# An encoder kernel's opening on a transposed input, weight differences one block earlier, and a last quarter in two column halves

## The chip, the cores and the metric

One core of one Trainium2 chip. The metric is device time in microseconds of one execution: every input is in the chip's DRAM at the start, and the output must be there at the end.

## The reference

Two layers on 256 tokens of width 1024, all in float32. Each layer is a half-step feed-forward network (FFN), a mixing part with two attentions, and a second half-step FFN. The diff touches the FFNs, the opening ahead of the first and the end of the last; the mixing part is left as it was.

```python
D_MODEL, SEQ, DEPTH, D_FF = 1024, 256, 2, 2816

def rms_norm(x, g):
    return x * lax.rsqrt(jnp.mean(x * x, axis=-1, keepdims=True) + EPS) * g

def swiglu(x, w_gate, w_up, w_down):
    return (jax.nn.silu(x @ w_gate) * (x @ w_up)) @ w_down

for l in range(DEPTH):
    x = x + 0.5 * swiglu(rms_norm(x, ffn1_norm[l]), ffn1_w_gate[l], ffn1_w_up[l], ffn1_w_down[l])
    z = rms_norm(x, mix_norm[l]) @ w_in[l]
    ...
    x = x + merged @ w_out[l]
    x = x + 0.5 * swiglu(rms_norm(x, ffn2_norm[l]), ffn2_w_gate[l], ffn2_w_up[l], ffn2_w_down[l])
```

## The kernel before, in words

**Precision.** Every matrix is cut in a high part (rounded to the matmul's type) and a low part (the rest), and every product takes three matmuls: high by high, high by low, low by high (`three`, L193 to L196). ACT makes the high part by a copy, DVE the low part by a subtraction (`start_split`, L208 and L209). For weights these are `wh` and `wl`, made from a `raw` tile that a DMA brought; for activations `xh0`, `xl0` (tokens 0 to 127, "t0") and `xh1`, `xl1` (tokens 128 to 255, "t1").

**Norm.** The gain is multiplied into the transposed activations (`norm_steps`: four transposes on TensorE, a multiplication, a split). The scale of each token, 1/sqrt(mean square), is applied after the projection, when gate and up are combined: ACT computes the squares' sums (`square`), DVE two small steps on `ms`, POOL the power (`rs_y`, L200).

**An FFN** runs over 11 blocks of 512 columns (256 of gate, 256 of up). A block has 1024 rows of weights, in four pieces of two 128-row chunks each; TensorE takes 24 matmuls of 512 columns for each half of the tokens. `glu` (L480, L481) then computes the gating: ACT takes silu of the gate half, DVE multiplies by the up half, into `hh`. `send` turns `hh` over by a transposing DMA, `arrive` takes it back, adds and subtracts its quarters (tile `a`), and splits the result.

**Down projection.** Blocks are paired with their rows of the down matrix in a scheme with seven products of half the size instead of eight: names "1" to "7". Its weight side takes differences of the down matrix's rows (`sums`, tile `uv`, three instructions on DVE) and a split corner (`keep_corner`). The products of one pair, except "1", run among the matmuls of the block that follows (`quad`). The last blocks' rows are multiplied plainly at the end (`down_end`), a quarter of the output at a time: names "2", "3", "4" and "8".

**The first block of pairs** is block 3 of an FFN that opens a layer's first half (`first_quad`), and block 2 in the second FFN of a layer. The block ahead of it, c == first_quad - 1, fetches the first rows (`fetch_rows(0)`) and begins three pieces of the next block.

**The opening.** The first FFN of layer 0 has no earlier work to hide its loads. `opening` fetches x in four quarters, the gains of all norms in front of the first (HEAD columns), and block 0's four pieces. TensorE runs matmuls on a blank tile (`warmup`) between the first transposes.

**Order.** TensorE's order is the program's. The other engines' order comes from a scheduler that works with estimated times, except where `linked` ties an instruction behind the last one of the same engine in `chain`; between `chain[...] = ...` and `chain.clear()` a stretch of ACT's or DVE's work stands in the order in which it is written. `defer` holds a piece of work back until TensorE has done so many more units. SP issues the loads of weights and x in order, POOL the loads of small constants (`constants`, L105 to L107), behind the second norm's power. `behind` only sets an order between two loads.

**Buffers.** `raw` has 4, `wh` and `wl` 6 each, `rows` 2. The projection's PSUM tiles `g` have 2 banks.

Of the kernel before, what the change touches and what calls it, by code (L numbers as in the profile page):

```python
# [23 lines left out]
P = 128  # L24
# [27 lines left out]
IN_W = 4352  # L52
HEAD = 128
HELD = 3
# [5 lines left out]
@with_exitstack  # L60
def hybrid_encoder(ctx, tc, x, w_gu1, w_d1, w_in, b_gate, qk_gain, rpb, sink, t5,
                   w_bna, w_bsw, w_out, w_gu2, w_d2, c_mask, c_band, out):
# [17 lines left out]

    def fetch(t, h):
        if (t, h) == (0, 0):
            nc.sync.dma_start(wide[:, :HEAD + 512], x[:P, :HEAD + 512])
        else:
            nc.sync.dma_start(xs[t][:, h * 512:(h + 1) * 512],
                              x[t * P:(t + 1) * P, HEAD + h * 512:HEAD + (h + 1) * 512])

    fetch(0, 0)

# [44 lines left out]

    last_load, last_hi = [None], [None]

# [70 lines left out]
    def start_split(hi, lo, src):  # L207
        last_hi[0] = linked("act", lambda: nc.scalar.activation(hi, src, AF.Copy))  # L208
        return lambda: linked("dve", lambda: nc.vector.tensor_tensor(lo, src, hi.bitcast(F32), ALU.subtract))  # L209

    def split_to(hi, lo, src):
        start_split(hi, lo, src)()
# [6 lines left out]

    def norm_steps(t, n, half, apart=False):  # L220
        if half == 0:
            xT[t] = [act.tile([P, KD, P], F32R, name=f"x{p}{t}", tag=f"x{p}{t}") for p in "hl"]
            ssq[t] = small.tile([P, 2], F32, name="ssq", tag="ssq")
# [6 lines left out]
        if apart and half == 1:  # L230
            for i in range(4):
                linked("act", lambda: nc.scalar.activation(xg[:, i, :], tp[:, i, :], AF.Copy,
                                                           scale=gain[:, n, 4 + i:5 + i]))
        else:
            linked("dve", lambda: nc.vector.tensor_tensor(
                xg, tp, gain[:, n, ks].unsqueeze(2).to_broadcast([P, 4, P]), ALU.mult))
        yield
        split_to(*(x[:, ks, :] for x in xT[t]), xg)
        yield
        if not apart:  # L240
            square(t, half)

    def norm(t, n, half, apart=False):
        for _ in norm_steps(t, n, half, apart):
            pass
# [11 lines left out]

    def opening(w, l, early):
        ps = [ps_g.tile([P, 512], F32, name="g", tag="g") for _ in range(T)]

        def steps(t, i):
            wh, wl = pieces[i]
            xh, xl = xT[t]
            for a, b in ((xh, wh), (xl, wh), (xh, wl)):
                for k in (2 * i, 2 * i + 1):
                    nc.tensor.matmul(ps[t], a[:, k, :], b[:, k % 2, :], start=a is xh and b is wh and k == 0,  # L266
                                     stop=b is wl and k == KD - 1)
            tick(2)

        pieces = []  # L270
        chain["act"] = warmed
        warmup(5)
        norm(0, 0, 0, True)
        pieces.append(piece(w, l, 0, 0, 512))
        warmup(5)
        fetch(1, 0)
        norm(1, 0, 0, True)
        pieces.append(piece(w, l, 1, 0, 512))
        fetch(0, 1)
        fetch(1, 1)  # L280
        warmup(3)
        steps(0, 0)
        norm(0, 0, 1, True)
        steps(1, 0)
        pieces.append(piece(w, l, 2, 0, 512))
        norm(1, 0, 1, True)
        pieces.append(piece(w, l, 3, 0, 512))
        square(0, 0, idle)
        square(0, 1, idle)
        for i in (1, 2, 3):  # L290
            for t in range(T):
                steps(t, i)
        second = [piece(w, l, 0, 512, 512)]
        square(1, 0, idle)
        early(ps[0])
        second.append(piece(w, l, 1, 512, 512))
        square(1, 1, idle)
        second += [piece(w, l, i, 512, 512) for i in range(2, KD // 2)]
        chain.clear()
        defer(24, "constants", constants)  # L300
        defer(70, "scaled", scaled)
        return ps, second

# [52 lines left out]
    def ffn(l, n, w_gu, w_d, after, early, begun):  # L356
        first_quad = 2 if n else 3
        QUADS = NFC - first_quad
        with tc.tile_pool(name="ffn", bufs=1) as fp:
            on_way, rows_of, corner, hs, one = [], {}, {}, {}, {}  # L360

            def send(c, hh):
                z = fp.tile([P, 8 * P], U16, name="z", tag="z")
# [69 lines left out]
            def down_end(rest, start):  # L433
# [70 lines left out]
            for c in range(NFC):  # L504
                first = n == 0 and c == 0
                pair = [None]
                if first:
                    both, second = opening(w_gu, l, lambda ps: glu(0, ps, pair))
                    glu(1, both[1], pair)
                    send(c, pair[0])  # L510
                    continue
                if c < first_quad:
                    if n == 0 and c == 1:
                        pieces = second
                    else:
                        pieces = [*begun, *(piece(w_gu, l, i, c * 512, 512) for i in range(len(begun), KD // 2))]
                        begun = []
                if c < first_quad - 1:
                    for t in range(T):
                        glu(t, project(t, pieces, 512), pair)  # L520
                    send(c, pair[0])
                    continue
                if c == first_quad - 1:
                    fetch_rows(0)
                    chain["act"], chain["dve"] = glu(0, project(0, pieces, 512), pair)
                    tiles = []
                    for i in range(3):
# [15 lines left out]
                for j, (t, i) in enumerate(order):  # L543
                    steps(ps, t, i, tiles[i])
                    if j == 1:
                        uv = sums(q)
                        tile, low = start(c, 3)
# [5 lines left out]
                    elif j == 5:  # L553
                        rest = arrive()
                        got.update(block("74", uv[:, 2:, :]))
                        rest()
                        keep_corner(q)
                ahead_tiles = []
# [342 lines left out]

    def store(t, d):
        cols = slice(d * 512, (d + 1) * 512)
        nc.sync.dma_start(out[t * P:(t + 1) * P, cols], xs[t][:, cols])
# [99 lines left out]
```

## Time and the profile before

| | |
|---|---|
| median of three runs | 1052.75 us (1052.63 to 1052.95) |
| time of the profiled execution | 1054.04 us |
| span in its profile | 1052.3 us |
| busy: TensorE matmul, VectorE, ScalarE, GpSimd | 99%, 85%, 73%, 11% of the span |
| granted TensorE clock | 1.0 over the execution |
| DMA | 216.78 MB, mean 206 GB/s |

PE is TensorE's matmul, PEld its weight load, DVE VectorE, ACT ScalarE, POOL GpSimd, SP the engine that issues most loads. Times in the rows are microseconds from the span's start, the first number of a row of the timeline is when the instruction starts, the second how long it takes, and in square brackets is the time for which its engine stood idle just before, with what released it. A row with "x4" groups several instructions. The profiled execution took 1.7 us more than its span, and 1.3 us more than the runs' median.

### The profile page before, as it was taken

Reading aid. Unit: us, or ns where it says so; the run is one execution under the profiler, and the core shown is the slowest. Engines: PE = TensorE matmul, PEld = TensorE weight load, DVE = VectorE, ACT = ScalarE, POOL = GpSimd, SP = SyncE. Lnnn points to the kernel's source line nnn. Section 1 sums busy time; section 2 is a strip of 40 time slices with the busy share of each in tenths; the row PEclk is TensorE's granted clock in tenths of the full one; section 3 lists DMA queues with packets and bytes.
Section 4 is the critical chain, followed back from the end, with each engine's and each line's share of the span. In section 5 each row is a group of like instructions: output and inputs, shape, how many; then the busy total and the mean of one; then the engine's idle time right before and its main releaser. Section 6 shows DMA issues by size and latency. Waiting matters only on the chain.

```text
span 1052.3 us, 14228 instructions
## 1 busy us (share of the span) xinstructions
PE 1044.3 (99%) x4908; PEld 867.7 (82%) x4908; DVE 898.4 (85%) x1363; ACT 771.2 (73%) x1129; POOL 115.4 (11%) x118
## 2 busy tenths in 40 slices
PE   9999999999999999999999999999999999999998
PEld 7888888878888888888887888888888887888886
DVE  6699987789896789999769999887898866999985
ACT  6677875788777678777467877757887676887872
POOL 1000300244420000000000000004534000000000
PEclk9999999999999999999999999999999999999999
DMA  7977754665757667786475776537566567777651
GB/s 256 285 223 242 233 186 140 210 201 177 197 181 192 244 200 228 237 259 187 144 248 202 245 229 235 161 110 249 191 205 174 189 191 247 215 232 237 225 181 50
DMA packets 117512, 216.78 MB, mean 206 GB/s; under 512 B 62096, under 2 KB 68272, under 8 KB 117440
## 3 DMA queue, kind: packets, MB, share of 16 engines
q1 hardware_dynamic: 117248, 215.80, 64.7%
q8 instruction: 38, 0.62, 0.2%
q0 software_dynamic: 192, 0.08, 0.2%
q14 instruction: 34, 0.28, 0.1%
HBM read 201.15 MB, written 1.06 MB: 192 GB/s over the span
## 4 chain that ended last, share of the span: by engine, by line
PE 91%; DVE 3%; DMA 3%; ACT 2%; issue 1%; ACTq 0%; DVEq 0%
PE g L194 20%; PE g L195 20%; PE g L196 20%; PE m L194 6%; PE m L196 6%; PE m L195 6%; DVE wl L209 2%; PE sc L677 1%; PE po L712 1%; DMA zT<-z 1%; PE pt L698 1%; PE acc L195 1%; PE acc L194 1%; PE acc L196 1%; DMA raw<-in_w_gu 1%; PE g L266 1%
## 5 line engine op out<-in xcount | busy, mean ns | idle before, releaser
L209 DVE TENSOR_TENSOR wl<-raw,wh 128x1024 fp32r<-128x1024 f32 (+1 forms) x296 | 355.3, 1220 | 33.6 <-ACT wh L208 33.2
L194 PE MATMUL g<-wh,xh 128*128 128x512 f32 (+1 forms) x976 | 381.8, 391 | 0.0
L195 PE MATMUL g<-wl,xh 128*128 128x512 f32 (+1 forms) x976 | 377.7, 387 | 0.9 <-DVE wl L209 0.9
L196 PE MATMUL g<-wh,xl 128*128 128x512 f32 (+1 forms) x976 | 377.2, 386 | 0.6 <-DVE xl L209 0.6
L208 ACT ACTIVATE wh<-raw 128x1024 fp32r<-128x1024 f32 (+1 forms) x296 | 304.7, 1039 | 24.4 <-PE g L196 8.9
L196 PEld LDWEIGHTS g<-wh,xl 128*128 128x128 f32 x976 | 183.4, 188 | 39.0 <-DVE xl L209 1.0
L195 PEld LDWEIGHTS g<-wl,xh 128*128 128x128 f32 x976 | 183.6, 188 | 35.6 <-DVE wl L209 2.5
L194 PEld LDWEIGHTS g<-wh,xh 128*128 128x128 f32 x976 | 183.5, 188 | 34.4 <-DVE hh L481 0.7
L208 ACT ACTIVATE wh<-uv 128x1024 fp32r<-128x1024 f32 x70 | 73.8, 1055 | 68.8 <-DVE uv L397 68.8
L194 PE MATMUL m<-wh,hi 128*128 128x512 f32 x274 | 107.2, 391 | 0.0
L196 PE MATMUL m<-wh,lo 128*128 128x512 f32 x274 | 106.7, 389 | 0.0
L195 PE MATMUL m<-wl,hi 128*128 128x512 f32 x274 | 106.6, 389 | 0.0
L209 DVE TENSOR_TENSOR wl<-uv,wh 128x1024 fp32r<-128x1024 f32 x70 | 85.5, 1222 | 1.0 <-ACT wh L208 1.0
L481 DVE SCALAR_TENSOR_TENSOR hh<-g,rs_y,hh 128x256 f32<-128x256 f32 x88 | 42.3, 480 | 41.6 <-ACT hh L480 39.1
L200 POOL TENSOR_TENSOR rs_y<-ms,mhalf 128x1 f32<-128x1 f32 x12 | 9.6, 807 | 544.8 <-DVE ms L255 544.8
L352 ACT ACTIVATE a<-zT 128x1024 uint16<-128x1024 uint16 x44 | 59.9, 1362 | 8.8 <-DMA zT<-z 8.6
L480 ACT ACTIVATE hh<-g,rs_y 128x256 f32<-128x256 f32 x88 | 41.0, 466 | 29.1 <-PE g L196 26.9
L196 PEld LDWEIGHTS m<-wh,lo 128*128 128x128 f32 x274 | 51.4, 188 | 10.9
L194 PEld LDWEIGHTS m<-wh,hi 128*128 128x128 f32 x274 | 51.4, 188 | 10.5
L195 PEld LDWEIGHTS m<-wl,hi 128*128 128x128 f32 x274 | 51.5, 188 | 10.5
L346 ACT ACTIVATE z<-hh 128x1024 uint16<-128x1024 uint16 x44 | 46.1, 1048 | 7.5 <-DMA zT<-z 5.3
L208 ACT ACTIVATE hi<-a 128x768 fp32r<-128x768 f32 (+1 forms) x44 | 35.4, 804 | 21.8 <-DVE a L380 21.6
(162 smaller groups left out, 1390.7 us busy)
## 6 DMA issues: line engine op xcount, KB each, us to landing
raw<-in_w_gu SPq DMA_DIRECT2D x176, 512.0 KB, 5.2
rows<-in_w_d SPq DMA_DIRECT2D x70, 512.0 KB, 4.4
raw<-in_w_in SPq DMA_DIRECT2D x64, 512.0 KB, 4.8
raw<-in_w_d SPq DMA_DIRECT2D x18, 512.0 KB, 4.0
raw<-in_w_out SPq DMA_DIRECT2D x16, 512.0 KB, 4.0
bb<-in_b_gate SPq DMA_DIRECT2D x16, 256.0 KB, 3.5
raw<-in_w_bsw SPq DMA_DIRECT2D x8, 512.0 KB, 3.9
raw<-in_w_bna SPq DMA_DIRECT2D x8, 512.0 KB, 3.5
```

Of the source, the lines that this page charges most:

```text
L194: nc.tensor.matmul(ps, xh, wh, start=first, stop=False)
L195: nc.tensor.matmul(ps, xh, wl, start=False, stop=False)
L196: nc.tensor.matmul(ps, xl, wh, start=False, stop=last)
L208: last_hi[0] = linked("act", lambda: nc.scalar.activation(hi, src, AF.Copy))
L209: return lambda: linked("dve", lambda: nc.vector.tensor_tensor(lo, src, hi.bitcast(F32), ALU.subtract))
L266: nc.tensor.matmul(ps[t], a[:, k, :], b[:, k % 2, :], start=a is xh and b is wh and k == 0, stop=b is wl and k == KD - 1)
L346: linked("act", lambda: nc.scalar.activation(z.rearrange("p (two n) -> p two n", two=2), src.bitcast(U16).rearrange("p s (n two) -> p two ...
L352: return linked("act", lambda: nc.scalar.activation(a.bitcast(U16).rearrange("p s (n two) -> p two (s n)", two=2), zT.rearrange("p (two s) ...
L480: silu = linked("act", lambda: nc.scalar.activation(h, gate, AF.Silu, scale=rstd[t]))
L481: return silu, linked("dve", lambda: nc.vector.scalar_tensor_tensor(h, up, rstd[t], h, op0=ALU.mult, op1=ALU.mult))
L677: nc.tensor.matmul(ps[:, t, :], qT[:, h, t * P:(t + 1) * P], k[:, kidx(h), :], start=i == 0, stop=i == 1)
L698: nc.tensor.transpose(tp[:, kt, t, :], S_[:, t, kt * P:(kt + 1) * P], ident)
```

## The change

1. **The opening takes x from a second, transposed copy.** `x_turned` (written on the host) has the gains in its first 64 columns and then eight chunks of 128 rows of x transposed. Each chunk's half is cut straight from the loaded tile: ACT writes the high part (a copy scaled by the gain), DVE the low part. The 16 transposes go, and 13 blank matmuls become 7. The first weight piece is fetched and split in two halves of 256 KB. x itself, still needed for the squares and for the residual, comes in two loads of 512 KB among block 1's pieces. Block 0 and block 1 each take both halves of the tokens piece by piece; block 1's two sums lie in PSUM tiles `next`. ACT's and DVE's instructions up to block 1's last piece stand in a tied order.
2. **The first pair's differences** (`sums(0)`, `keep_corner(0)`) and the first piece of the next block are made at c == first_quad - 1 ahead of the gating, in a tied order that begins behind the last split; for later pairs they stay where they were. This is so in all four FFNs.
3. **The last quarter of the output** ("8") is computed in two halves of 256 columns, each with its own sum and its own store.

`send`'s tile `z` now has two buffers.

```diff
-HEAD = 128
+HEAD = 64
...
     def start_split(hi, lo, src):
         last_hi[0] = linked("act", lambda: nc.scalar.activation(hi, src, AF.Copy))
...
+        def low():
+            last_lo[0] = linked("dve", lambda: nc.vector.tensor_tensor(lo, src, hi.bitcast(F32), ALU.subtract))
...
-    def opening(w, l, early):
+    def opening(w, l, early, home):
...
+        def fetch_turned(i):
+            nc.sync.dma_start(home[:, i, :], x_turned[:, HEAD + 512 * i:HEAD + 512 * (i + 1)])
+        def fetch(t):
+            behind(nc.sync.dma_start(xs[t], x[t * P:(t + 1) * P, :]), last_load[0])
+        def scale(k):
+            i = k // 2
+            src = (home[:, i, :] if i else wide[:, HEAD:HEAD + 512])[:, k % 2 * S:k % 2 * S + S]
+            g = gain[:, 0, k:k + 1]
+            for t in range(T):
+                cols = src[:, t * P:(t + 1) * P]
+                xh, xl = (a[:, k, :] for a in xT[t])
+                linked("act", lambda: nc.scalar.activation(xh, cols, AF.Copy, scale=g))
+                linked("dve", lambda: nc.vector.scalar_tensor_tensor(xl, cols, g, xh.bitcast(F32), op0=ALU.mult,
+                                                                     op1=ALU.subtract))
...
         chain["act"] = warmed
+        warmup(7)
+        raw = ring.tile([P, 2, 512], F32, name="raw", tag="raw", bufs=RAW)
+        src = w[l, :2 * P * 512].rearrange("(p k n) -> p k n", p=P, k=2)
+        for k in range(2):
+            last_load[0] = nc.sync.dma_start(raw[:, k, :], src[:, k, :])
+        raws = []
+        for i in range(1, KD // 2):
+            fetch_turned(i)
+            raws.append(fetch_piece(w, l, i, 0, 512))
...
+        for k in range(2):
+            scale(k)
+            split_to(wh[:, k, :], wl[:, k, :], raw[:, k, :])
+            steps((k,))
+        for i in range(1, KD // 2):
+            scale(2 * i)
+            scale(2 * i + 1)
+            pieces.append(parts(raws[i - 1]))
+            if i < 3:
+                steps((2 * i, 2 * i + 1))
+        steps((6, 7))
+        second = [piece(w, l, 0, 512, 512)]
+        fetch(0)
         square(0, 0, idle)
         square(0, 1, idle)
+        second.append(piece(w, l, 1, 512, 512))
+        early(0, ps[0])
+        fetch(1)
+        second.append(piece(w, l, 2, 512, 512))
         square(1, 0, idle)
         square(1, 1, idle)
+        early(1, ps[1])
+        second.append(piece(w, l, 3, 512, 512))
         chain.clear()
...
+                if n == 0 and c == 1:
+                    ps = [ps_acc.tile([P, 512], F32, name="next", tag="sc", bufs=2) for _ in range(T)]
+                    for i in range(KD // 2):
+                        for t in range(T):
+                            steps(ps, t, i, pieces[i])
+                    for t in range(T):
+                        glu(t, ps[t], pair)
...
                 if c == first_quad - 1:
+                    chain["act"], chain["dve"] = last_hi[0], last_lo[0]
                     fetch_rows(0)
-                    chain["act"], chain["dve"] = glu(0, project(0, pieces, 512), pair)
                     tiles = []
...
+                    uv = sums(0)
+                    keep_corner(0)
+                    prepare(0)
+                    glu(0, project(0, pieces, 512), pair)
+                    prepare(1)
+                    prepare(2)
                     rest = arrive()
                     glu(1, project(1, pieces, 512), pair)
...
-                    for t, d, name in ((0, 1, "3"), (1, 0, "4"), (1, 1, "8")):
+                    for t, d, name in ((0, 1, "3"), (1, 0, "4")):
                         plain(t, d, name)
                         after(t, d)
+                    for a, b in ((0, 256), (256, 512)):
+                        ps = ps_g.tile([P, 512], F32, name="m8", tag="g", bufs=2)[:, :b - a]
+                        for i, (wh, wl) in enumerate(rest):
+                            x = [h[:, (0, 3)[i % 2], :] for h in hs[QUADS + i // 2]]
+                            three(ps, *x, wh[:, 1, a:b], wl[:, 1, a:b], i == 0, i == len(rest) - 1)
+                        to = xs[1][:, 512 + a:512 + b]
+                        linked("dve", lambda: nc.vector.scalar_tensor_tensor(to, ps, 0.5, to, op0=ALU.mult,
+                                                                             op1=ALU.add))
+                        after(1, 1, a, b)
```

`prepare(i)` starts piece i of the next block and splits it. The later `sums(q)` and `keep_corner(q)` stand behind an `if q:`.

**Loads at the start.** SP's queue, from its first row. `x0` is the tile of t0's tokens (with the gains), `raw` a weight piece, `turned` a quarter of the transposed x. Before, and then now:

```order
L83 DMA x0_80<-in_x 128x640
L153 DMA raw_126<-in_w_gu1 128x1024
L85 DMA x1_81<-in_x 128x512
L153 DMA raw_150<-in_w_gu1 128x1024
L85 DMA x0_80<-in_x 128x512
L85 DMA x1_81<-in_x 128x512
L153 DMA raw_185<-in_w_gu1 128x1024
L153 DMA raw_203<-in_w_gu1 128x1024
L153 DMA raw_252<-in_w_gu1 128x1024
L153 DMA raw_262<-in_w_gu1 128x1024
L153 DMA raw_274<-in_w_gu1 128x1024
L153 DMA raw_280<-in_w_gu1 128x1024
```

```order
L81 DMA x0_80<-in_x_turned 128x576
L287 DMA raw_123<-in_w_gu1 128x512 x2
L258 DMA turned_107<-in_x_turned 128x512
L146 DMA raw_127<-in_w_gu1 128x1024
L258 DMA turned_107<-in_x_turned 128x512
L146 DMA raw_130<-in_w_gu1 128x1024
L258 DMA turned_107<-in_x_turned 128x512
L146 DMA raw_133<-in_w_gu1 128x1024
L146 DMA raw_233<-in_w_gu1 128x1024
L261 DMA x0_80<-in_x 128x1024
L146 DMA raw_247<-in_w_gu1 128x1024
L261 DMA x1_81<-in_x 128x1024
```

The four loads of x stood ahead of block 0's last two pieces; now the transposed x and the pieces take turns, and x itself follows behind block 1's first piece (x0) and its second (x1).

**DVE around block 2's pieces.** `hh` is a gating, `qkg` and `nsnk` are constants that come by POOL's loads, the `wl` are block 2's pieces. Before, and then now:

```order
L209 TENSOR_TENSOR wl_354<-raw_351,wh_353 128x1024
L481 SCALAR_TENSOR_TENSOR hh_259<-g_108,rs_y_272,hh_259 128x2x128
L111 SCALAR_TENSOR_TENSOR qkg_94<-qkg_94 128x2 x2
L209 TENSOR_TENSOR wl_360<-raw_357,wh_359 128x1024
L481 SCALAR_TENSOR_TENSOR hh_317<-g_292,rs_y_214,hh_317 128x256
L209 TENSOR_TENSOR wl_366<-raw_363,wh_365 128x1024
L113 TENSOR_SCALAR nsnk_97<-snk_96 128x16
L209 TENSOR_TENSOR wl_372<-raw_369,wh_371 128x1024
```

```order
L204 TENSOR_TENSOR wl_344<-raw_341,wh_343 128x1024
L104 SCALAR_TENSOR_TENSOR qkg_94<-qkg_94 128x2 x2
L204 TENSOR_TENSOR wl_350<-raw_347,wh_349 128x1024
L106 TENSOR_SCALAR nsnk_97<-snk_96 128x16
L204 TENSOR_TENSOR wl_356<-raw_353,wh_355 128x1024
L508 SCALAR_TENSOR_TENSOR hh_332<-next_282,rs_y_245,hh_332 128x256
L204 TENSOR_TENSOR wl_362<-raw_359,wh_361 128x1024
```

`nsnk` stood ahead of the fourth piece (`wl_372`) and now stands ahead of the third (`wl_356`); block 1's two gatings, `hh_317` and now `hh_332`, moved as well.

**DVE and ACT around the block ahead of the pairs** (the first FFN of layer 0; block 2's gating is `hh_406` and now `hh_409`). DVE before, and then now:

```order
L481 SCALAR_TENSOR_TENSOR hh_406<-g_378,rs_y_214,hh_406 128x256
L209 TENSOR_TENSOR wl_412<-raw_409,wh_411 128x1024
L209 TENSOR_TENSOR wl_418<-raw_415,wh_417 128x1024
L209 TENSOR_TENSOR wl_424<-raw_421,wh_423 128x1024
L209 TENSOR_TENSOR one0_429<-a_427,one0_429 128x128
L380 TENSOR_TENSOR a_427<-a_427 128x128 x4
L481 SCALAR_TENSOR_TENSOR hh_406<-g_438,rs_y_272,hh_406 128x2x128
L209 TENSOR_TENSOR lo_437<-a_427,hi_436 128x768
L397 TENSOR_TENSOR uv_488<-rows_375 128x2x512
L397 TENSOR_TENSOR uv_488<-rows_375,uv_488 128x512 x2
L209 TENSOR_TENSOR wl_495<-raw_492,wh_494 128x1024
```

```order
L508 SCALAR_TENSOR_TENSOR hh_332<-next_283,rs_y_268,hh_332 128x2x128
L415 TENSOR_TENSOR uv_368<-rows_365 128x2x512
L415 TENSOR_TENSOR uv_368<-rows_365,uv_368 128x512 x2
L204 TENSOR_TENSOR corner0_372<-rows_365,corner0_372 128x512
L204 TENSOR_TENSOR wl_378<-raw_375,wh_377 128x1024
L508 SCALAR_TENSOR_TENSOR hh_409<-g_381,rs_y_245,hh_409 128x256
L204 TENSOR_TENSOR wl_415<-raw_412,wh_414 128x1024
```

The three `uv` instructions and the corner's low part stood behind the block's second gating; now they stand ahead of its first, and the next block's first piece (`wl_378`) with them. ACT before, and then now:

```order
L480 ACTIVATE hh_317<-g_320,rs_y_272 128x2x128
L346 ACTIVATE z_347<-hh_317 128x1024
L480 ACTIVATE hh_406<-g_378,rs_y_214 128x256
L208 ACTIVATE wh_411<-raw_409 128x1024
L208 ACTIVATE wh_417<-raw_415 128x1024
L208 ACTIVATE wh_423<-raw_421 128x1024
L352 ACTIVATE a_427<-zT_289 128x2x512
L208 ACTIVATE one0_429<-a_427 128x128
L480 ACTIVATE hh_406<-g_438,rs_y_272 128x2x128
```

```order
L201 ACTIVATE wh_361<-raw_359 128x1024
L507 ACTIVATE hh_332<-next_283,rs_y_268 128x2x128
L201 ACTIVATE corner0_372<-rows_365 128x512
L364 ACTIVATE z_337<-hh_332 128x1024
L201 ACTIVATE wh_377<-raw_375 128x1024
L507 ACTIVATE hh_409<-g_381,rs_y_245 128x256
L201 ACTIVATE wh_414<-raw_412 128x1024
```

The corner's high part and the first `wh` of block 3 now stand ahead of the gating of block 2's first half.

More of the change, by code (lines that the diff above doesn't have):

```diff
@@ L218, in hybrid_encoder, with places, norm_steps @@
     ssq = [None] * T
-    def norm_steps(t, n, half, apart=False):
+    def places(t):
+        xT[t] = [act.tile([P, KD, P], F32R, name=f"x{p}{t}", tag=f"x{p}{t}") for p in "hl"]
+        ssq[t] = small.tile([P, 2], F32, name="ssq", tag="ssq")
+    def norm_steps(t, n, half):
         if half == 0:
-            xT[t] = [act.tile([P, KD, P], F32R, name=f"x{p}{t}", tag=f"x{p}{t}") for p in "hl"]
-            ssq[t] = small.tile([P, 2], F32, name="ssq", tag="ssq")
+            places(t)
         ks = slice(4 * half, 4 * half + 4)
@@ L229, in norm_steps @@
         xg = act.tile([P, 4, P], F32, name="xg", tag="xg", bufs=2)
[L230 to L236, printed above, removed]
+        linked("dve", lambda: nc.vector.tensor_tensor(
+            xg, tp, gain[:, n, ks].unsqueeze(2).to_broadcast([P, 4, P]), ALU.mult))
         yield
@@ L239, in norm_steps, with norm @@
         yield
[L240 to L244, printed above, removed]
+        square(t, half)
+    def norm(t, n, half):
+        for _ in norm_steps(t, n, half):
             pass
@@ L256, in square, with steps @@
             rstd[t] = rsqrt(v, 1)
-    def opening(w, l, early):
+    def opening(w, l, early, home):
         ps = [ps_g.tile([P, 512], F32, name="g", tag="g") for _ in range(T)]
[L261 to L270, printed above, removed]
-        chain["act"] = warmed
[L272 to L287, printed above, removed]
+        for t in range(T):
+            places(t)
+        def fetch_turned(i):
[12 more added lines that the diff above has]
+                                                                     op1=ALU.subtract))
+        def steps(ks, ts=range(T)):
+            for a, b in ((0, 0), (1, 0), (0, 1)):
+                for k in ks:
+                    for t in ts:
+                        nc.tensor.matmul(ps[t], xT[t][a][:, k, :], pieces[k // 2][b][:, k % 2, :],
+                                         start=k == 0 and a + b == 0, stop=k == KD - 1 and b == 1)
+            tick(len(ts) * len(ks))
+        chain["act"] = warmed
+        warmup(7)
[7 more added lines that the diff above has]
+            raws.append(fetch_piece(w, l, i, 0, 512))
+        wh, wl = (ring.tile([P, 2, 512], F32R, name="w" + p, tag="w" + p, bufs=RING) for p in "hl")
+        pieces = [(wh, wl)]
+        for k in range(2):
[11 more added lines that the diff above has]
+        fetch(0)
@@ L301, in opening @@
         defer(70, "scaled", scaled)
-        return ps, second
+        return second
     def project(t, pieces, n):
@@ L507, in ffn @@
                 if first:
-                    both, second = opening(w_gu, l, lambda ps: glu(0, ps, pair))
-                    glu(1, both[1], pair)
+                    home = fp.tile([P, 4, 512], F32, name="turned", tag="rows", bufs=2)
+                    second = opening(w_gu, l, lambda t, ps: glu(t, ps, pair), home)
                     send(c, pair[0])
@@ L517, in ffn @@
                         begun = []
+                if n == 0 and c == 1:
[3 more added lines that the diff above has]
+                            steps(ps, t, i, pieces[i])
+                    for t in range(T):
+                        glu(t, ps[t], pair)
+                    send(c, pair[0])
+                    continue
                 if c < first_quad - 1:
@@ L556, in ffn @@
                         rest()
[L557 removed]
+                        if q:
+                            keep_corner(q)
                 ahead_tiles = []
```

40 lines of the change are left out of this document (15 added, 25 removed).

## The prediction

> **What bounds the kernel now.** I read the page's busy shares first, then TensorE's instructions in order of time for gaps, then, at each gap and at both ends, what the engine was waiting for. "Pieces" are 512 KB weight tiles: two 128-row chunks of 512 columns, cut by ACT into `wh` and by DVE into `wl`. Block 0 is the first 512 columns of the first FFN's gate/up matrix, block 1 the next, and so on; each block takes 48 matmuls, from block 3 on with 18 more of a down-projection pair.
>
> ```profile
> PE 1044.3 (99%) x4908; PEld 867.7 (82%) x4908; DVE 898.4 (85%) x1363; ACT 771.2 (73%) x1129; POOL 115.4 (11%) x118
> ...
> 8.28 0.62 PE L266 MATMUL g<-wh,xh 128*128 128x512 f32 x2
> 20.32 0.45 PE L194 MATMUL g<-wh,xh 128*128 128x512 f32 x1
> 57.61 0.39 PE L194 MATMUL g<-wh,xh 128*128 128x512 f32 x1
> 58.28 0.50 PE L195 MATMUL g<-wl,xh 128*128 128x512 f32 x1 [0.29 <-DVE wl L209]
> 566.75 0.39 PE L196 MATMUL m<-wh,lo 128*128 128x512 f32 x1
> 566.98 0.42 PE L194 MATMUL g<-wh,xh 128*128 128x512 f32 x1
> 568.03 0.50 PE L195 MATMUL g<-wl,xh 128*128 128x512 f32 x1 [0.64 <-DVE wl L209]
> 568.37 0.39 PE L196 MATMUL g<-wh,xl 128*128 128x512 f32 x1
> 1048.39 0.69 DVE L426 SCALAR_TENSOR_TENSOR x<-m,x 128x512 f32<-128x512 f32 x1 [2.03 <-PE m L196]
> ```
>
> TensorE is the bound nearly everywhere: starts lie 0.227 us apart (566.75, 566.98). So time can come only from the opening (useful work starts at 8.28, block 1 at 20.32), from the few gaps, and from the end. Between 20.32 and 57.61, the first matmul of block 4, stand 162 matmuls, 36.7 us of work, so 0.6 us of gaps. At 58.28 TensorE waits 0.44 us for a `wl`, and its next start is 0.1 late: 0.55. At 568.03 the same place of layer 1's first FFN loses 0.82 and 0.11: 0.93. The last sum, 0.69 us, and its store end the span.
>
> **The opening.** Before, x is transposed on TensorE (16 transposes) ahead of the splits; now it arrives transposed, each of its 16 chunk halves is cut by one ACT and one DVE instruction, and the first piece comes in two halves.
>
> ```profile
> L153 SPq DMA_DIRECT2D raw<-in_w_gu x1: 416/416/416, 1.2 to 1.2; - x1
> DMA to landing us min/median/max: 4.1/4.1/4.1
> ...
> L153 SPq DMA_DIRECT2D raw<-in_w_gu x1: 431/431/431, 2.1 to 2.1; - x1
> DMA to landing us min/median/max: 6.2/6.2/6.2
> ...
> L153 SPq DMA_DIRECT2D raw<-in_w_gu x2: 443/470/498, 3.6 to 4.1; - x2
> DMA to landing us min/median/max: 7.3/7.7/8.0
> 3.00:12.00 9.00, 9.00 (x39) 6.91 (x38) 5.07 (x6) 4.33 (x9) 0.00 (x0) 1.00 1.01 365
> 12.39 1.05 ACT L208 ACTIVATE wh<-raw 128x1024 fp32r<-128x1024 f32 x1
> 13.34 1.12 ACT L232 ACTIVATE xg<-tp,x 128x128 f32<-128x128 f32 x4
> ```
>
> The DMA share is 1.01 from 3 to 12 us: loads set the pace. The four pieces land at 5.3, 8.3, 10.9 and 12.1, after 832, 1600, 2624 and 3136 KB. The new order has 288 KB, two halves of 256, then three times 256 of x and a 512 piece. By those points of KB against time the first piece is complete at 5.2 (800 KB), piece 1 at 8.2 (1568), piece 2 at 10.2 (2336), piece 3 at 12.1 (3104). The first half piece, about 0.7 us ahead of 5.2, and an ACT split near 0.6 start useful matmuls at 5.2. Twelve take 2.7, to 7.9. Then TensorE waits for piece 1: split 8.3 to 9.35, start 9.45. The other 36 take 8.2: ACT has four x chunks (1.1) and a split (0.95 to the next start) to do for each piece and ends `wh` of piece 3 at 13.3, needed at 14.9. The opening ends at 17.6 instead of 20.3: 2.7 us won, most of it because a half piece, not a whole one, starts it. The extra x chunks cost TensorE nothing while that 1.6 us of ACT slack lasts.
>
> **What is late next.** x itself must still come (1 MB, for the squares of the norm and the residual), now among block 1's pieces: these five transfers before block 1's third piece has landed take 5 x 1.44 us (512 KB at 365 GB/s), 12.1 to 19.3. ACT's tied order puts the squares of x1 behind that piece, and the constants' DMAs on POOL stand behind the second norm's power:
>
> ```profile
> 16.72 0.60 ACT L250 ACTIVATE idle<-x 128x512 f32<-128x512 f32 x1
> 17.25 0.19 ACT L250 ACTIVATION_READ_ACCUMULATOR idle<-x 128x1 f32 x1
> 17.91 0.55 POOL L200 TENSOR_TENSOR rs_y<-ms,mhalf 128x1 f32<-128x1 f32 x1 [16.60 <-DVE ms L255]
> 18.42 1.23 DVE L209 TENSOR_TENSOR wl<-raw,wh 128x1024 fp32r<-128x1024 f32 x1 [0.60 <-ACT wh L208]
> 22.23 3.49 DVE L209 TENSOR_TENSOR wl<-raw,wh 128x1024 fp32r<-128x1024 f32 x3
> 22.23 1.63 POOL L200 TENSOR_TENSOR rs_y<-ms,mhalf 128x1 f32<-128x1 f32 x1 [3.78 <-DVE ms L255]
> 23.82 0.79 POOL L105 DMA_DIRECT2D qkg<-in_qk_gain  x1
> 25.17 0.55 POOL L107 DMA_DIRECT2D snk<-in_sink  x1
> 32.62 0.17 DVE L113 TENSOR_SCALAR nsnk<-snk 128x16 f32<-128x16 f32 x1 [1.21 <-DMA snk<-in_sink]
> qkg<-in_qk_gain POOLq DMA_DIRECT2D x1, 4.0 KB, 4.7
> snk<-in_sink POOLq DMA_DIRECT2D x1, 8.0 KB, 7.4
> ```
>
> DVE runs in order, and in the new order `nsnk` stands ahead of `wl` of block 2's third piece, where before it stood ahead of the fourth. Before, DVE's wait at 32.6 was free, since that piece was due only at about 35.9 (block 2 began near 31.8). Now TensorE reaches it at 17.6 + 10.9 (block 1) + 2.7 + 0.2 = 31.4. The constant: third piece at 19.3, split to 20.3, two squares of 0.72 each (16.72 to 17.44) to 21.8, DVE's two small steps 0.35, power 0.55, so `qkg` is issued at 22.8, `snk` 1.35 later at 24.15, and with its lag of 7.4 lands at 31.55. `nsnk` (0.1 to the next start) and `wl` (1.23) give 32.9: TensorE waits 1.5, and 0.2 more at the fourth piece. Block 4 begins at 17.6 + 36.7 + 1.7 = 56.0: the opening brings 1.6 net. Bounds: a lag of 4.7 (`qkg`'s row) ends the wait, 3.3 net; `snk` no earlier than before (32.6) makes it 2.75, 0.55 net.
>
> The power took 0.55 while DVE stood still and 1.63 while it ran splits; now the next DVE instruction waits for that power, so I take 0.55. The Trainium skill, GPSIMD Engine Reference, section "Key points", says that POOL shares its SBUF interfaces with VectorE and is held up by instructions with two SBUF inputs; the trace agrees (0.55 against 1.63). With 1.63 the forecast below would be 1050.3.
>
> **Differences ahead.** `sums(0)` and `keep_corner(0)` move one block earlier in all four FFNs.
>
> ```profile
> 39.20 0.48 DVE L481 SCALAR_TENSOR_TENSOR hh<-g,rs_y,hh 128x256 f32<-128x256 f32 x1 [4.88 <-ACT hh L480]
> 46.66 1.22 DVE L397 TENSOR_TENSOR uv<-rows 128x1024 f32<-128x1024 f32 x1
> 47.91 1.42 DVE L397 TENSOR_TENSOR uv<-rows,uv 128x512 f32<-128x512 f32 x2
> 565.54 0.68 DVE L209 TENSOR_TENSOR corner<-rows,corner 128x512 fp32r<-128x512 f32 x1
> L153 SPq DMA_DIRECT2D raw<-in_w_gu x1: 376/376/376, 877.8 to 877.8; - x1
> DMA to landing us min/median/max: 7.7/7.7/7.7
> ...
> 891.37 0.47 ACT L480 ACTIVATE hh<-g,rs_y 128x256 f32<-128x256 f32 x1 [3.36 <-PE g L196]
> ```
>
> They are 1.22 + 1.42 + 0.68 = 3.3 us of DVE, taken out of the stretch that made `wl` 0.44 and 0.82 late, and put where DVE idled 4.9 us ahead of the gating (39.20's row). Both gaps go: 0.55 + 0.93. What is queued behind them: ACT now has `corner` and the next block's first split ahead of the second half's gating. The tightest place is the last FFN: that piece, issued at 877.8, landed 7.7 us later, at 885.5. Its split ends at 886.6 and lets the gating go, whose PSUM bank is wanted only when block 1's second half starts, just before 891.37. I cost it at nothing; the cover is some 4 us, and beyond it each us of late load is one of TensorE's.
>
> **The end.** 24 half-width matmuls replace 12.
>
> ```profile
> 200.52 0.28 PE L195 MATMUL g<-wl,xh 128*128 128x256 f32 x1
> 201.12 0.28 PE L194 MATMUL g<-wh,xh 128*128 128x256 f32 x1
> out<-x SPq DMA_DIRECT2D x4, 256.0 KB, 2.0
> ```
>
> Five starts of 256 columns take 0.60, 0.12 each: 2.88 against 2.72, 0.16 lost; the last one is 0.11 shorter (0.28 against 0.39); the sum takes 0.48 (the 128x256 form at 39.20) instead of 0.69. The store of half the bytes saves between 0 and 0.36 (128 KB at 365 GB/s); I take 0.2, since the row holds issue and completion too. Together 0.4, bounds 0.15 to 0.55. The first half's store, issued about 1.3 us before, is hidden.
>
> **Sum.** 1.6 + 0.55 + 0.93 + 0.4 = 3.5. The profiled span of 1052.3 (time 1054.04) becomes 1048.8 (1050.5). The runs' median stands 1.3 below the profiled execution's time, so 1052.75 - 3.5 = 1049.2.
>
> **Rivals.**
> - No wait on `snk`: its lag falls to 4.7 as `qkg`'s. For it: fewer loads stand in line at 24 us than before at 25; against: `snk` was the longest lag of the three. Opening 3.3 net, time 1047.5. The Trainium skill, DMA: Bandwidth & Descriptors, section "Queues, rings and completion order", says an engine takes turns between queue rows packet by packet; by that rule the lag hangs on SP's load at that moment; no run here shows it apart.
> - `snk` no earlier than before (slower x loads, or the power at 1.63): 0.55 net, time 1050.3.
> - The differences do not carry the two gaps (ACT, not DVE, ends last there): 1.48 less, 1050.7. Against: DVE's split began at its predecessor's end in both.
> - Slower: the two x loads and the burst after them hold `snk` so long that the wait eats everything. Each us of lag past 7.4 costs one; it decides at 7.4 + 3.5 = 10.9 us, and for 0.2% at 13.0: 1055. The longest lag in these rows is 8.0.
>
> **Chances.** A measurement tells 0.2% (2.1 us) from no change. Forecast (wait of 0.5 to 2.4 us, 1048.2 to 1050.2) 0.52; no wait 0.20; `snk` as before 0.16 (a third of it beyond 1050.65); differences without effect 0.08; slower 0.04 (half past 0.2%). Faster 0.85, same 0.13, slower 0.02. Range: from no wait with the end at its best, 1047.2, to past the late `snk`, 1050.9.
>
> **What would show it.** First useful matmul near 5.2, a gap to about 9.4, block 1 near 17.6, a gap of 1 to 2 us in block 2 with `nsnk` just before it, none at block 4 and in layer 1, last matmul to end 0.4 shorter. Wrong if block 1's pieces come late (a gap between 20 and 28) or if `snk` lands past 34.

## The result, and the profile after

| | before | after |
|---|---|---|
| median | 1052.72 us (1052.35 to 1053.98, 6 runs) | 1047.35 us (1046.87 to 1047.58, 6 runs) |
| ratio | | 0.9948 (0.9938 to 0.9958) |
| profiled execution, span | 1054.04, 1052.3 | 1047.57, 1045.5 |

5.4 us less (4.4 to 6.5 by the interval), against a forecast of 3.5. The time is that of the rival "no wait on `snk`", 1047.5, and there was no such wait. That the number agrees so well is partly luck: the opening brought less than the 3.3 us of that rival, and gaps that the forecast had left alone went as well (table below).

The first rows are from the page of after: busy shares, and section 4's chain. The two that follow are groups by line, the multiplications by `wl` before and after; the last column is the idle time ahead of them.

```profile
PE 1038.9 (99%) x4898; PEld 865.8 (83%) x4898; DVE 900.0 (86%) x1375; ACT 774.7 (74%) x1134; POOL 114.9 (11%) x118
PE 99%; DMA 1%; SPq 0%; ACT 0%; DVE 0%; issue 0%
...
L188 PE MATMUL g<-wl,xh 128*128 128x512 f32 (+1 forms) x960 | 370.9, 386 | 0.0
```

```profile
L195 PE MATMUL g<-wl,xh 128*128 128x512 f32 (+1 forms) x976 | 377.7, 387 | 0.9 <-DVE wl L209 0.9
```

In these products TensorE waits for no `wl` any more, and the chain to the end is 99% TensorE. Next, after in order of time: the opening, block 2's constants, the differences, block 4's first matmuls, and the end.

```profile
4.78 1.20 PE L278 MATMUL g<-wh,xh 128*128 128x512 f32 x2
8.46 0.63 PE L278 MATMUL g<-wl,xh 128*128 128x512 f32 x2
10.40 1.19 PE L278 MATMUL g<-wh,xh 128*128 128x512 f32 x4 [1.31 <-ACT wh L201]
18.70 0.39 PE L187 MATMUL next<-wh,xh 128*128 128x512 f32 x1
22.22 0.55 POOL L193 TENSOR_TENSOR rs_y<-ms,mhalf 128x1 f32<-128x1 f32 x1 [4.13 <-DVE ms L249]
22.73 0.79 POOL L98 DMA_DIRECT2D qkg<-in_qk_gain  x1
24.08 0.54 POOL L100 DMA_DIRECT2D snk<-in_sink  x1
28.23 0.17 DVE L106 TENSOR_SCALAR nsnk<-snk 128x16 f32<-128x16 f32 x1
28.31 1.22 DVE L204 TENSOR_TENSOR wl<-raw,wh 128x1024 fp32r<-128x1024 f32 x1
32.86 1.23 DVE L415 TENSOR_TENSOR uv<-rows 128x1024 f32<-128x1024 f32 x1 [1.08 <-DMA rows<-in_w_d]
55.42 0.39 PE L187 MATMUL g<-wh,xh 128*128 128x512 f32 x1
55.65 0.39 PE L188 MATMUL g<-wl,xh 128*128 128x512 f32 x1
1042.41 0.42 DVE L495 SCALAR_TENSOR_TENSOR x<-m,x 128x256 f32<-128x256 f32 x1 [1.01 <-PE m L189]
```

```profile
qkg<-in_qk_gain POOLq DMA_DIRECT2D x1, 4.0 KB, 4.2
snk<-in_sink POOLq DMA_DIRECT2D x1, 8.0 KB, 3.2
...
out<-x SPq DMA_DIRECT2D x2, 128.0 KB, 1.7
```

Useful work starts at 4.78, waits 1.31 (1.48 beyond the pitch) for the second piece's split, and block 1 begins at 18.70. From there to 55.42 it is 36.7 us of matmuls without a gap: `snk` was issued when forecast (24.08) but landed after 3.2 us, at 27.3, and `nsnk` stood ahead of the third piece's `wl` without a wait. Where the two profiles part, matched matmul by matmul:

| place | won, us | forecast |
|---|---|---|
| start of block 1 (20.32 to 18.70) | 1.6 | 2.7 |
| gaps from block 1 to block 4 | 0.6 | 0.6 |
| wait on `snk` | 0 | -1.7 |
| differences, layers 0 and 1 | 0.6 + 1.0 | 0.55 + 0.93 |
| end (3.87 to 3.04 from the last sum to the span's end, less 0.16) | 0.67 | 0.4 |
| gaps elsewhere: mix of layer 0 (0.94), end of layer 1's mix (0.33), its last FFN (0.95), 0.19 before layer 1's block 4 | 2.4 | none |

These sum to the 6.8 us between the spans. The medians differ by 5.4: the profiled execution of before was itself 1.3 above its median, that of after 0.2.

### The profile page after: what moved, and what is told of

Same layout as the page of the kernel before. It is cut to its first block, busy times and chain, and to the rows that moved or that the text cites. A ratio compares the mean times of both kernels' runs of the same rounds, so it can differ in the third digit from the quotient of the medians.

```text
span 1045.5 us, 14211 instructions
## 1 busy us (share of the span) xinstructions
PE 1038.9 (99%) x4898; PEld 865.8 (83%) x4898; DVE 900.0 (86%) x1375; ACT 774.7 (74%) x1134; POOL 114.9 (11%) x118
## 4 chain that ended last, share of the span: by engine, by line
PE 99%; DMA 1%; SPq 0%; ACT 0%; DVE 0%; issue 0%
PE g L187 21%; PE g L189 21%; PE g L188 21%; PE m L187 7%; PE m L189 7%; PE m L188 7%; PE sc L723 1%; PE po L758 1%; PE acc L187 1%; PE acc L189 1%; PE acc L188 1%; PE pt L744 1%; PE tp L228 1%; PE g L278 1%; PE br L188 1%; PE br L187 1%
## 5 line engine op out<-in xcount | busy, mean ns | idle before, releaser
L187 PE MATMUL g<-wh,xh 128*128 128x512 f32 (+1 forms) x960 | 375.2, 391 | 0.0
L188 PE MATMUL g<-wl,xh 128*128 128x512 f32 (+1 forms) x960 | 370.9, 386 | 0.0
L189 PE MATMUL g<-wh,xl 128*128 128x512 f32 (+1 forms) x960 | 370.8, 386 | 0.0
L189 PEld LDWEIGHTS g<-wh,xl 128*128 128x128 f32 x960 | 180.4, 188 | 37.4
L188 PEld LDWEIGHTS g<-wl,xh 128*128 128x128 f32 x960 | 180.6, 188 | 32.9
L187 PEld LDWEIGHTS g<-wh,xh 128*128 128x128 f32 x960 | 180.5, 188 | 32.8
L187 PE MATMUL m<-wh,hi 128*128 128x512 f32 (+1 forms) x278 | 108.0, 388 | 0.0
L189 PE MATMUL m<-wh,lo 128*128 128x512 f32 (+1 forms) x278 | 107.4, 386 | 0.0
L188 PE MATMUL m<-wl,hi 128*128 128x512 f32 (+1 forms) x278 | 107.4, 386 | 0.0
L415 DVE TENSOR_TENSOR uv<-rows,uv 128x512 f32<-128x512 f32 x70 | 48.4, 692 | 2.3
```

Source lines behind the costliest of these rows:

```text
L187: nc.tensor.matmul(ps, xh, wh, start=first, stop=False)
L188: nc.tensor.matmul(ps, xh, wl, start=False, stop=False)
L189: nc.tensor.matmul(ps, xl, wh, start=False, stop=last)
L415: linked("dve", lambda: nc.vector.tensor_tensor(to, x, y, ALU.subtract))
```

## The experiments

Before and after stand for the two kernels; times beside a run are medians, with before's on the same chip.

**The parts alone.** `again` is before unchanged.

> The kernel before, unchanged, profiled once more. In its first profile TensorE lost 1.07 us at 210.59 and 0.77 + 0.11 at 879.56, each at a weight piece that landed late; the changed kernel's profile has neither, and no part of the change works there. Theory A (the lateness of a load differs from one execution to the next): this profile lacks at least one of the two, or has it smaller by half, and its span lies nearer 1051 than 1052.3; the gaps of 0.55 and 0.93 at the differences stay. Rival B (these gaps belong to the order of before, and the change took them away): both stand at the same places within 0.2 us, span 1052.3.

> Before with part 3 alone (the last quarter in two column halves). By the changed kernel's trace the end is 0.66 us shorter. Theory A: 0.4 to 0.7 us faster, about 1052.1 against 1052.7, and nothing before the last quarter moves beyond what differs between executions. Rival (the store's completion sets the end whatever its size): 0.2 or less.

> Before with part 2 alone (the first pair's differences ahead of the gating). Theory A: the gaps at block 4 of both layers' first FFN go, 1.5 us faster, about 1051.2. Rival B (the tied order also brings the late pieces of the mix and of the last FFN in time): 2.5 us or more, below 1050.3. Rival C (ACT ends last at these places): under 0.5.

> Before with part 1 alone (the transposed opening, one z buffer more). The changed kernel's trace has block 1 at 18.7 and no gap in block 2. Theory A: 2.2 us faster, about 1050.5, and the gap at block 4 stays, 0.4 to 0.7. Rival B (the loads that the opening lets start earlier bring the late pieces of the mix in time too): 3.2 us or more, below 1049.6. Rival C (without the differences ahead the wait for snk appears after all): under 1.2.

The edits, each against before:

```diff
 # tail: part 3 of the diff, nothing else
 # diffs: part 2
 # opening: part 1 and z's second buffer
```

| | median | before | ratio |
|---|---|---|---|
| `again` (one run) | 1051.4 | 1052.61 | |
| `tail` | 1051.99 | 1052.61 | 0.9997 (0.9988 to 1.0006) |
| `diffs` | 1051.64 | 1052.61 | 0.9992 (0.9984 to 1.0001) |
| `opening` | 1049.87 | 1052.61 | 0.9975 (0.9967 to 0.9984) |

Before spread from 1051.28 to 1054.47 over 27 runs, after from 1046.87 to 1047.58 over 6. The profile of `again` shows what spreads: the gap near 210 is 0.40 us instead of 1.07, that near 878 0.29 instead of 0.77, and the two that part 2 takes away are smaller by 0.33 and 0.61, where theory A had them stay. In `tail`, with the old order, both of these are gone. So the forecast's 1.48 for part 2 was read from an execution at the upper end; alone it measured 1.0 (0.8 by the ratio, and not certain to be a gain). `diffs` so fell between its theories A (1.5) and C (under 0.5), and `opening`, 2.7 faster, between A (2.2) and B (3.2 or more). The gap that part 2 is for was largest in the profile of `opening`; at block 4, timeline:

```profile
55.24 0.43 PE L187 MATMUL g<-wh,xh 128*128 128x512 f32 x1
56.30 0.50 PE L188 MATMUL g<-wl,xh 128*128 128x512 f32 x1 [0.63 <-DVE wl L204]
```

It loses 0.83 there, 0.82 at layer 1's place and 0.91 at the block behind it. In none of the nine profiles with the differences ahead is there a gap at block 4; with the old order four of five have one, of 0.1 to 0.8. `diffs` had one of 0.86 elsewhere, at 25.85 in block 1, so it gave part back in its profiled execution. The three alone sum to 4.3; the whole gives 5.4, and the intervals do not set these apart.

**The gap in the last FFN.** Theory A of `again` held for the size of the gaps, not for their place: the gap near 878 was in all four profiles with the old opening (0.77, 0.29, 0.59, 0.78) and in neither of the two with the new one (after and `opening`). The load behind it is the same in each, the first that SP issues after a pause. In before it landed at 877.5, and ACT, DVE and TensorE waited for it in turn:

```profile
877.58 1.06 ACT L208 ACTIVATE wh<-raw 128x1024 fp32r<-128x1024 f32 x1 [2.50 <-DMA raw<-in_w_gu]
879.82 0.68 DVE L209 TENSOR_TENSOR xl<-xg,xh 128x512 fp32r<-128x512 f32 x1
880.56 0.50 PE L196 MATMUL g<-wh,xl 128*128 128x512 f32 x1 [0.59 <-DVE xl L209]
```

The `xl` that TensorE needs stands behind that piece's `wh` and `wl` on ACT and DVE. The next rows are that load's time to landing and, from the view of DMA queues, what else moved in its window; first before, then `opening`.

```profile
L153 SPq DMA_DIRECT2D raw<-in_w_gu x1: 328/328/328, 872.4 to 872.4; - x1
DMA to landing us min/median/max: 5.1/5.1/5.1
...
q1 hardware_dynamic: 287, 1.06, 58.7%
q8 instruction: 1, 0.02, 1.1%
```

```profile
L146 SPq DMA_DIRECT2D raw<-in_w_gu x1: 328/328/328, 870.5 to 870.5; - x1
DMA to landing us min/median/max: 3.5/3.5/3.5
...
q1 hardware_dynamic: 180, 0.67, 56.0%
```

Before has one packet of kind "instruction" in that window (queue q8, 16 KB), `opening` none. To move it with nothing but blank matmuls (in `phase_after` `nsnk` also came behind one more split):

```diff
+    def tiny(n):
+        for _ in range(n):
+            nc.tensor.matmul(idle[:, :16], blank[:, 0, :P], blank[:, 0, :16], start=True, stop=True)
-        warmup(5)        # phase_before; in phase_after warmup(7)
+        warmup(3)
+        tiny(37)         # phase_after: tiny(39)
```

> Before, with 2 of the 13 blank matmuls at the start replaced by 37 blank ones of 16 columns: 35 more matmul and weight-load pairs ahead of everything, nothing else moved. In four profiles with the old opening one packet of 16 KB of kind 'instruction' (queue q8, one every 28 us or so, 38 in all) lay inside the load of the last FFN's second piece of block 1 and the load took 4.6 to 5.1 us; in the two with the new opening it lay elsewhere and the load took 3.4 to 3.5. Theory A (the fetch of TensorE's instructions takes one of the 16 DMA engines for about 1 us, and its place hangs on the count of TensorE's instructions): 35 pairs move it 8 us earlier, the load near 871 takes 3.3 to 3.7, the gap near 878 (0.3 to 0.8 in four profiles) is at most 0.1, and the median is 0.3 to 0.9 below before's. Rival (the load is late for another reason): the gap stays, median within 0.2 of before's.

> The changed kernel, with 4 of its 7 blank matmuls replaced by 39 blank ones of 16 columns: the same 35 pairs more; nsnk moves behind one more split. Theory A: the packet of kind 'instruction' lands in the load that decides in the last FFN (near 868), that load takes 4.5 to 5.1 us instead of 3.4, a gap of 0.3 to 0.8 appears near 873, and the median rises to 1047.7 to 1048.3 from 1047.35. Rival: no gap there, median within 0.2.

Both medians missed (1058.75 and 1053.62): a matmul of 16 columns took 0.21 us, not the fraction of 0.43 that had been counted on, and put the start of block 1 off by 7.7 and 6.2 us. The places can still be read. `phase_before`: the load of the last FFN, and then the same load of layer 0's second FFN, with its window's queues and the gap behind it.

```profile
L157 SPq DMA_DIRECT2D raw<-in_w_gu x1: 328/328/328, 878.8 to 878.8; - x1
DMA to landing us min/median/max: 3.5/3.5/3.5
```

```profile
L157 SPq DMA_DIRECT2D raw<-in_w_gu x1: 328/328/328, 360.1 to 360.1; - x1
DMA to landing us min/median/max: 5.2/5.2/5.2
...
q8 instruction: 1, 0.02, 1.1%
...
368.36 0.50 PE L200 MATMUL g<-wh,xl 128*128 128x512 f32 x1 [0.61 <-DVE xl L213]
```

The gap left the last FFN and came up in layer 0's second FFN, 0.78 beyond the pitch, where no other profile has one, and the packet with it. In `phase_after` the packet began 0.7 us ahead of the load, not in it; the load took 3.4 and there is no gap, so that run did not test the theory. Over all fourteen profiles (this load in both second FFNs, 28 in all), the five that a packet of q8 fell into took 4.6 to 5.2 us, the 23 others 3.3 to 3.6. Eight of these others overlapped with a packet of 8 KB of the same kind on queue q14, mostly at their start, and were not late. So the new opening, with fewer instructions of TensorE ahead of these packets, took 0.3 to 0.9 us out of the last FFN: a gain that no line of the change is about, and that another change of the count may undo. (That the packets carry TensorE's instructions is inferred: 35 more pairs of matmul and weight load at the start, 8 us of work, moved one 9.6 us earlier against the load, and there are 38 packets in every run of 4886 to 4920 matmuls, 39 in the two of 4933 and 4943.) The gap near 210 (0 to 1.07 over the profiles) follows no such rule that I found and stays open.

**The start.** Block 0's second piece landed later than forecast.

> The changed kernel with the transposed x stored as four contiguous pieces instead of one wide matrix with rows of 8448 bytes; nothing else. In the changed kernel block 0's pieces landed about 1 us later than the forecast had them (6.7, 9.3, 11.1, 13.1 instead of 5.2, 8.2, 10.2, 12.1), nearly all of it lost from 4.1 to 6.7 us. Theory A (the start of any load sequence is slow, whatever its rows; before had 219 GB/s in its sixth microsecond too): landings within 0.2 us, block 1 at 18.6 to 18.8, median within 0.2 of 1047.35. Rival (reads of 2 KB with a stride of 8448 bytes are slow): landings 0.5 to 1.0 earlier, block 1 at 17.7 to 18.2, median 0.5 to 1.0 lower.

> The changed kernel with block 0's second piece also fetched, split and multiplied in two halves. In the changed kernel TensorE stood still 1.48 us from 8.9 to 10.4 for that piece's split. Theory A (the wait is for the whole piece's landing and its 1.06 us split): the first half lands near 8.6, its split takes 0.6, TensorE goes on near 9.3, then waits once more, 0.3 to 0.6, for the third piece; block 1 begins 0.5 to 0.9 earlier and the median is 1046.4 to 1046.9. Rival (ACT, which has 24 splits of x and weights here, ends last at the third piece, so the wait only moves there): block 1 within 0.2 of 18.7, median within 0.2 of 1047.35.

> The changed kernel once more, timed and profiled beside the three that follow. Block 1 began at 18.7 in its first profile, at 18.5 with part 1 alone, at 17.7 with the x pieces contiguous and at 17.4 with the second piece in halves, whose loads before that piece were the same as here and yet landed 0.6 earlier. Theory A (strided x costs landing time, and some of the difference is the execution): block 1 at 18.2 to 18.8, median 1047.0 to 1047.6. Rival (all of it is the execution): block 1 at 17.5 to 18.1.

> The changed kernel with the contiguous x pieces and the second piece in halves together. Each alone came to 1046.8. Theory A (they act at different places, landing and split): block 1 at 16.5 to 17.1, one gap of 0.3 to 0.8 ahead of the second piece and at most 0.5 at the third, median 1046.0 to 1046.5. Rival (both only move the start of the second piece, and the third piece's landing and split end last): block 1 at 17.2 to 17.5, median 1046.6 to 1046.9.

> The changed kernel with block 0's first piece as one load and one split of 512 KB. The forecast laid most of the opening's gain on the half pieces. Theory A (the second piece's landing ends last, so an earlier start of the first is idle time moved): the first useful matmul moves from 4.8 to 6.7 to 7.6, the idle time ahead of the second piece falls to 0 to 0.5, block 1 and the median stay within 0.3 of the changed kernel's. Rival (the half pieces bring the start and the end of the opening alike): block 1 1.0 or more later, median 1048.3 or more.

```diff
 # contig: x_turned stored piece by piece (its first load, and the array on the host, likewise)
-            nc.sync.dma_start(home[:, i, :], x_turned[:, HEAD + 512 * i:HEAD + 512 * (i + 1)])
+            nc.sync.dma_start(home[:, i, :], x_turned[P * (HEAD + 512 * i):P * (HEAD + 512 * (i + 1))].rearrange("(p n) -> p n", p=P))
 # halves1: piece 1 as piece 0 (its loads likewise in two)
+                for k in range(2):
+                    split_to(wh1[:, k, :], wl1[:, k, :], raw1[:, k, :])
+                    steps((2 + k,))
 # whole: piece 0 as one load
+        raw = fetch_piece(w, l, 0, 0, 512)
 # both: contig and halves1;  after_again: after
```

| | block 1 at | second piece landed | median | before |
|---|---|---|---|---|
| after, first profile | 18.70 | 9.3 | 1047.35 | 1052.72 |
| `after_again` | 17.21 | 7.8 | 1046.82 | 1052.69 |
| `contig` | 17.70 | 8.2 | 1046.83 | 1052.55 |
| `halves1` | 17.39 | 8.0, 8.7 (halves) | 1046.73 | 1052.55 |
| `both` | 16.99 | 7.7, 8.3 (halves) | 1047.21 | 1052.69 |
| `whole` | 17.51 | 8.0 | 1046.62 | 1052.69 |

The same load in two executions of the same kernel, first after, then `after_again`, and what it made of the opening in the second:

```profile
L146 SPq DMA_DIRECT2D raw<-in_w_gu x1: 432/432/432, 2.6 to 2.6; - x1
DMA to landing us min/median/max: 6.7/6.7/6.7
```

```profile
L146 SPq DMA_DIRECT2D raw<-in_w_gu x1: 432/432/432, 2.6 to 2.6; - x1
DMA to landing us min/median/max: 5.2/5.2/5.2
...
8.91 1.20 PE L278 MATMUL g<-wh,xh 128*128 128x512 f32 x4
17.21 0.39 PE L187 MATMUL next<-wh,xh 128*128 128x512 f32 x1
```

1.5 us apart with nothing changed: the rival of `after_again` holds, block 1 starting even earlier than the rival had it, and no run shows a cost of the stride of the x pieces. `contig` had seemed to bear its rival out; one profile each could not tell. `halves1` and `both` begin block 1 as early as hoped and `whole` between the two profiles of after, all without a median that differs from `after_again`'s. In `whole` the first useful matmul moved to 5.6, sooner than expected, and the opening ended no later than in after: an earlier start of the first piece was idle time moved. `both` had gaps of 0.42 in block 3, where TensorE waited for block 2's second gating, and of 0.76 at 206.7 in its profiled execution. None of these beats after clearly.

**The wait on `snk`.**

> The changed kernel with the constants held back by six idle powers on POOL (0.55 to 1.0 us each), so that qkg is issued near 26 to 28.7 and snk near 27.5 to 30; qkg's two products and nsnk are tied ahead of the low split of block 2's third piece, as nsnk was. The idle powers are no part of the result. In the changed kernel snk was issued at 24.1 and landed 3.2 us later, with one load of SP ahead of it; now four or more of SP's loads (25.5 to 26.9) are issued before it. Theory A (the forecast's mechanism holds, its lag was wrong: the lag grows with the loads in line, and nsnk's wait passes to TensorE): snk's lag is 5 to 8 us, it lands at 33.5 to 37, and TensorE waits at block 2's third piece from 32.3 until snk's landing plus 1.3 us, so 2.5 to 6 us, and the median rises by as much. Rival (the lag is 3 to 4 whatever SP does): snk at 30.7 to 33.5, TensorE waits 0 to 2.5. Second rival (nsnk's wait does not reach TensorE): no gap and no loss whatever the landing.

```diff
+        idler = const.tile([P, 8], F32, name="idler")
+        last = rstd_done[0]
+        for _ in range(6):
+            with tc.issue_after(last.ins):
+                last = nc.gpsimd.tensor_tensor(idler[:, :1], rstd[1], mhalf[:, :1], ALU.pow)
+        with tc.issue_after(last.ins):
             nc.gpsimd.dma_start(qkg, qk_gain)
...
-        defer(70, "scaled", scaled)
...
+                            if (l, n, c, i) == (0, 0, 2, 2):
+                                need("constants")
+                                chain["dve"] = scaled()
+                            pieces.append(piece(w_gu, l, i, c * 512, 512))
+                            chain.clear()
```

The rows of `late`: timeline of POOL, DVE and TensorE, the constant's time to landing, and two stretches of time (busy time of each engine, then the granted clock, DMA share and GB/s).

```profile
29.72 0.54 POOL L105 DMA_DIRECT2D snk<-in_sink  x1
36.70 0.17 DVE L111 TENSOR_SCALAR nsnk<-snk 128x16 f32<-128x16 f32 x1 [1.40 <-DMA snk<-in_sink]
36.78 2.35 DVE L209 TENSOR_TENSOR wl<-raw,wh 128x1024 fp32r<-128x1024 f32 x2
38.05 0.79 PE L193 MATMUL g<-wl,xh 128*128 128x512 f32 x1 [6.28 <-DVE wl L209]
38.65 0.63 PE L194 MATMUL g<-wh,xl 128*128 128x512 f32 x1
39.07 0.63 PE L192 MATMUL g<-wh,xh 128*128 128x512 f32 x1
...
snk<-in_sink POOLq DMA_DIRECT2D x1, 8.0 KB, 7.0
...
38.00:44.20 6.20, 6.15 (x15) 4.79 (x16) 5.87 (x7) 0.99 (x2) 0.00 (x0) 0.50 0.84 309
44.20:50.00 5.80, 5.80 (x27) 4.78 (x26) 3.92 (x9) 3.85 (x6) 0.00 (x0) 1.00 0.82 261
```

What SP issued around `snk` before (issued at 25.17), then now (24.08), and what SP had waited for (us, times, longest):

```profile
24.62 0.33 SPq L153 DMA_DIRECT2D raw<-in_w_gu  x1
25.00 0.91 SPq L388 DMA_DIRECT2D rows<-in_w_d  x2
```

```profile
25.52 0.33 SPq L146 DMA_DIRECT2D raw<-in_w_gu  x1
SPq L146 <- DVE wl L204: 3.4, 1, 3.4
```

Theory A holds: `snk` took 7.0 us with four of SP's loads and a transposing DMA under way, against 3.2 with one load, landed at 36.7, and TensorE went on 1.4 us later, having stood still for 6.4 beyond the pitch. (No run has the loads without the transposing DMA at this place; in before, where the lag was 7.4, that DMA was issued only at 30.29.) The median rose by more than that, to 1055.86 (before 1052.69): after the wait the granted clock was 0.50, and the 14 starts from 38.05 on lay 0.43 apart (0.59 behind the first) instead of 0.227, 3.0 us more; 6.4 and 3.0 make 9.4, and `late` stands 9.0 above `after_again`. The Trainium skill, TensorE: Matmul & The Clock Gate, "Part 1: The HAM clock gate", says that an idle window of some 3.4 us halves the clock until the engine has been busy for such a window; the trace agrees on the half, not on the times. Here the clock fell at 34.0, 2.2 us after the last matmul's end, and came back after 6.1 us of work.

## Why the prediction was right, and where it was not

- **The bound.** Right: TensorE, and only gaps and ends to win.
- **The start of block 1, 2.7 us.** The mechanism was right: the loads' landings set it. The size is the execution's: 1.6 in after's profile, 1.8 in `opening`, 2.5 in `late`, 3.1 in `after_again`. The step from KB to landing times took one profile's curve as fixed, and the same load moved by 1.5 us between executions: the first two pieces, forecast for 5.2 and 8.2, were complete at 6.7 and 9.3 in after's profile and at 5.4 and 7.8 in `after_again`. That the half piece does most of it was wrong: `whole` starts block 1 as early.
- **The wait on `snk`, 1.7 us.** This is the step that failed. The order, the issue (24.15 forecast, 24.08 measured; 22.85 in `after_again`) and the path to TensorE (`late`: landing plus 1.4) were right. The lag was not: 7.4 was carried over from before, where SP had issued two loads in the microsecond ahead of `snk` and a third 0.3 us behind it. Now SP issued nothing between 21.7 and 25.5: its next load waited 3.4 us for a `raw` buffer, which a `wl` split frees, so one load stood in line. The wait was also laid against a block 1 that starts at 17.6. By the forecast's own steps, a lag of 7.4 in after's profile would have cost an estimated 0.3 (24.08 + 7.4 + 1.33, against TensorE at 18.70 + 13.8). That the lag hangs on SP's load was in the rival; its chance was put at 0.20 because `snk` had been the longest of three, which says nothing about the new queue. What was drawn there from the Trainium skill, DMA: Bandwidth & Descriptors, "Queues, rings and completion order", agrees with 3.2 against 7.0 as far as the lag grows with SP's load; that an engine takes turns packet by packet no run shows.
- **The power at 0.55 while DVE stands still.** Right (22.22, 0.55).
- **Differences ahead, 1.48 us.** Right in place and in this pair of profiles; over executions the medians put it nearer 1.0, with an interval that includes no gain, since both gaps change from one execution to the next. The cover of the moved work held: of the nine profiles only `both` lost anything at the gating behind it (0.42).
- **The end, 0.4 us.** Low: the sum fell by 0.27, the store from 2.0 to 1.7, and 0.2 to 0.3 more lie between; 0.67 net, just past the bound of 0.55. `tail` alone gave 0.6, too little for its interval.
- **Left out.** The gaps in the mix and in the last FFN were taken to stay. They gave 2.4 us in this pair of profiles; what the medians owe them is not settled, since before's profile stood 1.3 above its median. Part of it, in the last FFN, comes from the place of the instruction packets.
- **The slower rival** did not occur: 3.2 us of lag, far from 10.9.

## What to carry to other kernels

Before a lag is carried over to a new order, see which queue it stood in and what will stand there now. A gap of half a microsecond in one profile is one draw: profile the unchanged kernel twice, and price the gap by both. Where a start waits for loads, cutting the first piece finer only moves the idle time unless the next piece comes sooner too.

## What the runs showed of the hardware

- Packets of kind "instruction" come on queue q8 in 16 KB (38 in a run of after, 0.62 MB, some 28 us apart) and took 0.9 to 2.2 us each; the one in before's window is 1.1% of 16 engines over 5.3 us, which is one engine for 0.9 us. A 512 KB load, otherwise alone, that one fell into took 4.6 to 5.2 us instead of 3.3 to 3.6.
- The first loads of an execution vary: the same piece landed at 7.8 us in `after_again` and at 9.3 in after's first profile.
- In `phase_after` matmuls of 16 columns took 0.21 us each, half as long as the 0.43 of those of 512 beside them, and 8 us of them did not end the slow start: the 12 starts behind them still lay 0.43 apart (the column of the granted clock reads 1.00 there).
